# Decoder block on one core: quarter sums on VectorE, and another order of the first stage

## The chip, the core and the metric

The kernel runs on one core of a Trainium2 chip. A core has five engines with an instruction stream each: TensorE (PE, the matrix engine), VectorE (DVE), ScalarE (ACT), GpSimd (POOL) and SyncE (SP), which here only issues DMAs. Each stream runs in order, and the engines wait for each other through semaphores. Time is device time of one execution in microseconds (us); the figure given for a kernel is the median of its runs.

## The reference

One decoder block over 512 tokens and 1024 features, in float32:

```python
cs = silu(c)
mod = cs @ ada_w + ada_b                      # 6 x 1024: shift, scale, gate; twice
h = rmsnorm(x, norm_mix_g) * (1 + sc_m) + sh_m
q, k, v, g_ret, b, c_cv, u, g_a, g_b = split(h @ w_in)        # each 512 x 1024
q = rope(q, cos, sin); k = rope(k, cos, sin) * 128 ** -0.5    # 8 heads of 128
y_ret = head_layernorm(retention(q, k, v))
y_a = (silu(g_ret) * y_ret) @ ret_w_out
y_b = (b * conv3(c_cv * u)) @ conv_w_out
x = x + gt_m * ((sigmoid(g_a) * y_a + sigmoid(g_b) * y_b) @ mix_w_out)
h = rmsnorm(x, norm_ffn_g) * (1 + sc_f) + sh_f
x = x + gt_f * ((silu(h @ ffn_w_gate) * (h @ ffn_w_up)) @ ffn_w_down)     # 2816 wide
out = rmsnorm(x, final_norm_g)
```

`cos` and `sin` are those of position times inverse frequency; `rope` makes `t1 cos - t2 sin` and `t1 sin + t2 cos` of the two halves of a head.

## The kernel before

**Products.** Every float32 operand is split into a high part (a cast on ACT, names ending in `_h`) and the low rest (a subtraction on DVE, `_l`), and a product is three matmuls into one accumulator, low by high, high by low, high by high (`mm3`). A 128-feature column block of a projection, over 8 blocks of depth, is 24 matmuls of 512 columns. Its first matmul reads the low part of the weight, so it needs DVE's subtraction.

**Stages.** First stage: `x_load` brings four tiles of 128 tokens, `x_squares` sums their squares on ACT (Square, then Sqrt), `x_scaled` divides by the root on DVE and transposes on PE; `mod_row` multiplies pieces of `ada_w` by `cs` on PE, `ada_sum` does the same on DVE into `acc_m`, and `mod_sums` adds DVE's share on PE. From that come scale and shift for the first blocks of h, `Hh` and `Hl` (high and low). Then the products of c, u, b and the first k block run together, one depth block after another as the modulation becomes ready. Up to line 577 every engine's order is as written (`strict` in the class `InTurn`: each instruction is emitted after the one before on its engine).

After that come the projections of v, k, q and the ret gate with rotation and retention, one pair of heads (`p`) after another, then conv, output projections (`p_ya`, `p_yb`) with their gates (`p_ga`, `p_gb`), the mix, the FFN and the last norm. There a scheduler sets the order: it lists instructions by its own estimate of when their inputs will be there. `tc.issue_after` orders emission and with it the scheduler's estimate; it does not by itself put a wait between two engines.

**The rotation.** `rotary_steps` reduces position times frequency to a fraction of a turn in a chain of small DVE instructions (`fr`, `fy`); `rope_tables` makes `ropeC` and `ropeS` of it with eight Sin activations; `rope` takes each finished accumulator (`p_k`, `p_q`) and computes `a = p * C`, `b` in two halves of 64 rows, `a + b`, then the split in `_h` and `_l`. The positions are loaded on POOL's queue (lines 154 to 157).

**Sums over partitions.** In several places a sum over 128 partitions is left as four sums over 32 (`quarter_sums`, DVE's transposing reduction). `quart_sum` is a constant 0/1 matrix with which a small matmul adds the four quarters and spreads the result: `mod_quarters` (first stage), `mod_whole` (scale and shift of the FFN norm, between the output projections), and `gate_vec.spread` (the two gate vectors). Constants `quart_sum`, `quart_own` are made by `quarters`.

In the trace nearly all instructions go through `InTurn` and so bear its lines L62 (strict) and L64 (not strict).

Of the kernel before, what the change touches and what calls it, by code (L numbers as in the profile page):

```python
# [11 lines left out]
F32 = mybir.dt.float32  # L12
# [3 lines left out]
AF = mybir.ActivationFunctionType  # L16
ALU = mybir.AluOpType
AX = mybir.AxisListType

P = 128  # L20
S = 512
D = 1024
# [48 lines left out]
def block_kernel(ctx, tc, x, c, positions, ada_w, ada_b, norm_mix_g, w_in, conv_w, ret_w_out,  # L71
# [3 lines left out]
    pe, vec, act, pool, sync = (InTurn(tc, e) for e in (nc.tensor, nc.vector, nc.scalar, nc.gpsimd,  # L75
                                                        nc.sync))
# [13 lines left out]
    def scr(name, dt=F32, shape=None):  # L90
        return tp.tile(shape or [P, S], dt, tag="scr", bufs=12, name=name)
# [7 lines left out]
    def aux(name, shape=None):  # L99
        return ps.tile(shape or [P, S], F32, tag="aux", bufs=2, name=name)  # L100
# [30 lines left out]

    HS = S // 2
    c_sb = cp.tile([P, KT], F32, name="c_sb")
    sync.dma_start(c_sb, c.rearrange("o (p k) -> (o p) k", p=P))
    rows = cp.tile([P, P], F32, name="rows")
    vec.memset(rows, 0.0)
    R_ADA, R_GM, R_GF, R_CW = 0, 48, 56, 64
# [11 lines left out]
    with tc.issue_after(pool.last.ins):  # L149
        small.dma_start(rows[0:48], ada_b.rearrange("o (r p) -> (o r) p", p=P))  # L150
        small.dma_start(rows[48:56], norm_mix_g.rearrange("o (r p) -> (o r) p", p=P))
        small.dma_start(rows[56:64], norm_ffn_g.rearrange("o (r p) -> (o r) p", p=P))
        small.dma_start(rows[64:88], conv_w.rearrange("o t (r p) -> (o t r) p", p=P))
        for i in range(2):
            small.dma_start(posi[64 * i:64 * i + 64],
                            positions[0, HS * i:HS * (i + 1)].partition_broadcast(64))
        small.dma_start(ivf, inv_freq.rearrange("(f o) -> f o", o=1))
# [1 line left out]
    x2 = x[0].rearrange("(t p) (h n) -> t h p n", p=P, n=S)  # L159

    cs = cp.tile([P, KT], F32, name="cs")
    act.activation(cs, c_sb, AF.Silu)
    warm = cp.tile([P, 1], F32, name="warm")
    with tc.issue_after(act.last.ins):
        act.activation(warm, eps_t, AF.Sqrt)

    onesr = cp.tile([P, P], F32R, name="onesr")

# [2 lines left out]
    def rows_by_feature(tr):  # L171
        vecs.append(cp.tile([P, P], F32, name="vecs"))
        act.copy(vecs[0], tr[:, 0:P])
# [62 lines left out]
    QP = P // 4  # L236
    quart, own, mod_q = {}, {}, {}

    def quarters():
        quart["sum"] = cp.tile([P, 4, QP], F32, name="quart_sum")  # L240
        cols = sp.tile([P, QP], F32, tag="quart", bufs=1, name="quart_cols")
        vec.tensor_reduce(cols, ident.rearrange("p (q c) -> p c q", q=4), axis=AX.X, op=ALU.add)
        vec.tensor_copy(quart["sum"], cols.unsqueeze(1).to_broadcast([P, 4, QP]))
        quart["own"] = cp.tile([P, 4], F32, name="quart_own")
        vec.tensor_reduce(quart["own"], ident.rearrange("p (q c) -> p q c", q=4), axis=AX.X,
                          op=ALU.add)
        quart["f"] = cp.tile([P, 2 * D // QP], F32, name="quart_f")
# [10 lines left out]
        quarter_sums(quart["f"][:, j // 2 * n:(j // 2 + 1) * n], a)  # L258

    def mod_whole():  # L260
        pt = aux("mod_f")[:, 0:2 * D // QP]
        mm(pt, lhsT=quart["sum"].rearrange("p q c -> p (q c)"), rhs=quart["f"], start=True,
           stop=True)
        each = scr("mod_each")[:, 0:2 * D // QP].rearrange("p (n q) -> p n q", q=4)
        vec.tensor_tensor(each, pt.rearrange("p (n q) -> p n q", q=4),
                          quart["own"].unsqueeze(1).to_broadcast([P, 2 * KT, 4]), ALU.mult)
        cols = sp.tile([P, KT // 2, 2, 2], F32, tag="quart", bufs=1, name="mod_cols")
        vec.tensor_reduce(cols.rearrange("p a s b -> p (a s b)"), each, axis=AX.X, op=ALU.add)
        a, b, s = (mod[f"{v}_f"].rearrange("p (a b) -> p a b", b=2) for v in "abs")
        g, r = (vecs[0][:, c:c + KT].rearrange("p (a b) -> p a b", b=2)  # L270
                for c in (R_GF, R_ADA + ADA["sh_f"] // P))
        vec.tensor_tensor(a, cols[:, :, 1], g, ALU.mult)
        vec.tensor_tensor(a, a, b, ALU.add)
        vec.tensor_tensor(s, cols[:, :, 0], r, ALU.add)
# [58 lines left out]
    def x_load():  # L333
        for t in range(NT):
            xt = wp.tile([P, 2, S], F32, tag="hi", name=f"x_{t}")
            xs[t] = [xt[:, h] for h in range(2)] + [xt.rearrange("p h n -> p (h n)")]
            load_raw.last = sync.dma_start(xs[t][2], x[0, t * P:(t + 1) * P, :])

    def w_load(k):
        for n in "cubk":  # L340
            cols = P if n == "k" else 2 * P
            w_raw[n, k] = scr(f"w_{n}0_{k}", F32, [P, 2, cols])
            load_raw.last = sync.dma_start(
                w_raw[n, k], wi[k * P:(k + 2) * P, COL[n]:COL[n] + cols].rearrange(
                    "(k p) n -> p k n", p=P))
# [17 lines left out]
    def x_squares(t):  # L363
        junk = scr(f"n1_{t}", BF16, [P, D])
        act.activation(junk, xs[t][2], AF.Square, accum_out=ssq[:, t:t + 1])
        act.activation(r4[:, t:t + 1], ssq[:, t:t + 1], AF.Sqrt, scale=1.0 / D, bias=eps_t)

    def x_scaled(t):
        r = r4[:, t:t + 1]
        vec.reciprocal(r, r)  # L370
        vec.tensor_scalar_mul(xs[t][2], xs[t][2], r)
        for h in range(2):
            txs[t, h] = acc(f"tx_{t}{h}").rearrange("p (k n) -> p k n", n=P)
            for k in range(4):
                transpose(txs[t, h][:, k], xs[t][h][:, k * P:(k + 1) * P], ident)
# [25 lines left out]
    busy(18)  # L401
    for t in range(2):
        x_squares(t)
    x_scaled(0)
    busy(3)
    x_squares(2)
# [3 lines left out]
    tr = pv("tr_rows")  # L410
    transpose(tr[:, 0:P], rows, ident)
    x_squares(3)
    rows_by_feature(tr)
    x_scaled(2)
    busy(1)
# [5 lines left out]
    x_by_feature(2, 0, act.copy)  # L421
    x_by_feature(2, 1, act.copy)
    mod_gains("m")
    quarters()
    mod_row(0, 1, apart, False)
    a = ada_sum(ada_raw["m", 0][2:6], 4 * P, "m0", None, 2)
    x_by_feature(3, 0, act.copy)
# [117 lines left out]
    for j in range(2, KT, 2):  # L545
        if j + 2 < KT:
            ada_load("m", j + 2)
            w_load(j + 2)
        steps = products(j - 1)
        run(steps, 14)  # L550
        if j == 2:
            mod_row(j, 7, both, True)
        else:
            some_sums(j, 4, KT)
        for n in "cubk":
            w_hi(n, j)
        if j < KT - 2:
            mod_sums(sums[j], both, j > 2)
            w_lo("c", j)
            mod_cols("m", j, mods.rearrange("p (i n) -> p i n", n=P)[:, :, 0])  # L560
        else:
            mod_quarters(j)
            w_lo("c", j)
            mod_own(j)
        for k in (j, j + 1):
            h_hi(k)
            h_full(k)
        for n in "ubk":
            w_lo(n, j)
        run(steps)  # L570
        some_sums(j + 2, 0, 2)
        h_lo(j)
        run(products(j))
        some_sums(j + 2, 2, 4)
        h_lo(j + 1)
# [316 lines left out]
    def gate_vec(name):  # L892
        gate[name] = [misc(f"{name}_{h}") for h in range(2)]
        bias = sp.tile([QP, QP], F32, tag="gbias", bufs=1, name=f"bias_{name}")
        nc.gpsimd.dma_start(
            bias, ada_b[0, ADA[name]:ADA[name] + D].rearrange("(j c) -> j c", c=QP))
        part = sp.tile([P, QP], F32, tag="gpart", bufs=1, name=f"part_{name}")

        def summed(j):
            raw = wp.tile([P, KT, 2 * P], F32, tag="raw", bufs=3, name=f"ada_{name}{j}")  # L900
            col = ADA[name] + 2 * j * P
            load_raw.last = nc.sync.dma_start(raw, aw[:, :, col:col + 2 * P])
            a = ada_sum([raw[:, k] for k in range(KT)], 2 * P, f"{name}{j}")
            n = 2 * P // QP
            quarter_sums(part[:, j * n:(j + 1) * n], a)

        def spread():

            pt = aux(f"gp_{name}")[0:QP, 0:QP]
            mm(pt, lhsT=quart["sum"][:, 0], rhs=part, start=True, stop=True)  # L910
            row = sp.tile([QP, QP], F32, tag="grow", bufs=1, name=f"row_{name}")
            vec.transpose(row, pt)
            vec.tensor_tensor(row, row, bias, ALU.add)
            line = dp.tile([QP, QP], F32, tag="gline", bufs=2, name=f"line_{name}")
            nc.gpsimd.dma_start(line, row)
            for h in range(2):
                nc.gpsimd.dma_start(
                    gate[name][h], line[h * QP // 2:(h + 1) * QP // 2].rearrange(
                        "j c -> (j c)").partition_broadcast(P))

        for j, n in enumerate((1, 3, 5, 6)):
            after(n, lambda j=j: summed(j))
        after(7, spread)
# [415 lines left out]
```

## Time and profile before

| | |
|---|---|
| median of 3 runs | 936.87 us (936.76 to 937.35) |
| profiled execution | 937.46 us, span of its trace 935.7 us |
| TensorE busy | 927.3 us, 4299 matmuls |
| VectorE busy | 623.9 us, 1001 instructions |
| ScalarE busy | 358.9 us, 531 instructions |
| GpSimd busy | 37.6 us, 72 instructions |
| HBM traffic | 139.91 MB read, 17.85 MB written |

How to read the lines that follow: a line of the timeline gives start, duration, engine, source line, operation, output and inputs with their shapes, and in brackets the idle time ahead of it and what ended it. A row of the windows gives the window, its length, then busy time (and instruction count) of PE, PE's weight loads, DVE, ACT and POOL, then the clock granted to PE (1.00 is full), the share of the DMA engines and GB/s. A row of the chain gives start, duration, engine and output. Consecutive matmuls overlap, so the distance of their starts (0.227 us for 512 columns, from 10.88 us for 48) is the price of one, not the 0.39 us of its row.

### The profile page before, as it was taken

How to read it: one execution, taken by the hardware profiler on the slowest of the kernel's cores; microseconds unless marked ns; L12 is line 12 of the kernel's file. 1: busy time of each engine (PE TensorE's matmuls, PEld its weight loads, DVE VectorE, ACT ScalarE, POOL GpSimd, SP SyncE). 2: the span in 40 equal slices, each digit the busy share in tenths (PEclk: the TensorE clock that was granted, in tenths of full speed). 3: DMA queues.
4: the chain of work that ended last, by engine and by line, in shares of the span. 5: the costliest groups of instructions: out<-in, count | busy, mean ns of one | idle time of the engine just before them, and what ended most of it. 6: DMA issues, size and time to landing. Idle time of an engine off the chain costs nothing.

```text
span 935.7 us, 11163 instructions
## 1 busy us (share of the span) xinstructions
PE 927.3 (99%) x4299; PEld 774.9 (83%) x4299; DVE 623.9 (67%) x1001; ACT 358.9 (38%) x531; POOL 37.6 (4%) x72
## 2 busy tenths in 40 slices
PE   8999999999999999999999999999999999999997
PEld 8888888888888888888888888988888888888886
DVE  5999784797868566654674457667665545566575
ACT  7534432544444333222233235423433223443324
POOL 2000000000001000000000000000011000001000
PEclk9999999999999999999999999999999999999999
DMA  9943423322463537765553552445578672368912
GB/s 324 338 156 107 136 73 102 102 72 98 153 218 102 180 103 244 215 203 191 170 190 113 180 181 89 136 152 190 198 248 269 225 255 72 102 168 233 334 63 90
DMA packets 119909, 158.49 MB, mean 169 GB/s; under 512 B 5476, under 2 KB 94864, under 8 KB 118704
## 3 DMA queue, kind: packets, MB, share of 16 engines
q1 hardware_dynamic: 114672, 139.61, 45.3%
q0 software_dynamic: 5040, 18.04, 6.0%
q8 instruction: 33, 0.54, 0.2%
q14 instruction: 20, 0.16, 0.1%
q10 hardware_dynamic: 144, 0.13, 0.0%
HBM read 139.91 MB, written 17.85 MB: 169 GB/s over the span
## 4 chain that ended last, share of the span: by engine, by line
PE 96%; DVE 1%; ACT 1%; DMA 1%; SPq 0%; issue 0%; DVEq 0%
PE p_fu L64 13%; PE p_fg L64 12%; PE dn_t L64 5%; PE p_g L64 5%; PE p_yb L64 5%; PE p_gb L64 5%; PE p_q L64 5%; PE p_v L64 5%; PE p_ya L64 5%; PE p_ga L64 5%; PE p_k L64 4%; PE dn_b L64 4%; PE p_b L64 4%; PE p_u L64 4%; PE p_c L64 3%; PE mix L64 3%
## 5 line engine op out<-in xcount | busy, mean ns | idle before, releaser
L64 PE MATMUL p_fu<-Gh,w_fu_l 128*128 128x512 f32 x160 | 62.4, 390 | 0.0
L64 PE MATMUL p_fu<-Gh,w_fu_h 128*128 128x512 f32 x160 | 62.3, 389 | 0.0
L64 PE MATMUL p_fu<-Gl,w_fu_h 128*128 128x512 f32 x160 | 62.2, 389 | 0.0
L64 PE MATMUL p_fg<-Gh,w_fg_l 128*128 128x512 f32 x160 | 62.2, 389 | 0.0
L64 PE MATMUL p_fg<-Gl,w_fg_h 128*128 128x512 f32 x160 | 62.2, 389 | 0.0
L64 PE MATMUL p_fg<-Gh,w_fg_h 128*128 128x512 f32 x160 | 62.2, 389 | 0.0
L64 DVE TENSOR_TENSOR w_bl<-w_bl 128x512 f32<-128x512 f32 x36 | 24.8, 688 | 26.7 <-DMA w_bl<-in_ffn_w_down_dram 26.4
L64 ACT CAST w_fu_h<-w_fu 128x1024 fp32r<-128x1024 f32 x20 | 21.0, 1054 | 56.2 <-PE p_fu L64 33.3
L64 DVE TENSOR_TENSOR w_fg_l<-w_fg,w_fg_h 128x1024 fp32r<-128x1024 f32 x20 | 24.3, 1219 | 25.3 <-ACT w_fg_h L64 25.2
L64 DVE TENSOR_TENSOR w_b_l<-w_b,w_b_h 128x1024 fp32r<-128x1024 f32 (+1 forms) x21 | 24.0, 1146 | 22.2 <-ACT w_b_h L64 22.1
L64 ACT ACTIVATE fg<-p_fg 128x512 f32<-128x512 f32 x22 | 13.1, 598 | 62.5 <-PE p_fg L64 62.5
L64 PEld LDWEIGHTS p_fu<-Gh,w_fu_h 128*128 128x128 f32 x160 | 30.0, 188 | 6.3
L64 PEld LDWEIGHTS p_fg<-Gh,w_fg_h 128*128 128x128 f32 x160 | 30.0, 188 | 6.3
L64 PEld LDWEIGHTS p_fu<-Gh,w_fu_l 128*128 128x128 f32 x160 | 30.0, 188 | 6.2
L64 PEld LDWEIGHTS p_fg<-Gh,w_fg_l 128*128 128x128 f32 x160 | 30.0, 188 | 6.2
L64 PEld LDWEIGHTS p_fg<-Gl,w_fg_h 128*128 128x128 f32 x160 | 30.0, 188 | 6.2
L64 PEld LDWEIGHTS p_fu<-Gl,w_fu_h 128*128 128x128 f32 x160 | 30.0, 188 | 6.2
L64 DVE TENSOR_TENSOR fg<-p_fu,fg 128x512 f32<-128x512 f32 x22 | 15.2, 690 | 27.8 <-PE p_fu L64 27.8
L64 DVE TENSOR_TENSOR w_t_l<-w_t,w_t_h 128x1024 fp32r<-128x1024 f32 (+1 forms) x20 | 22.2, 1115 | 13.9 <-ACT w_t_h L64 13.8
L64 ACT CAST w_t_h<-w_t 128x1024 fp32r<-128x1024 f32 (+1 forms) x20 | 19.4, 968 | 25.5 <-PE dn_t L64 12.7
L64 ACT CAST w_b_h<-w_b 128x1024 fp32r<-128x1024 f32 (+1 forms) x21 | 20.8, 989 | 20.4 <-issue 7.9
L64 ACT CAST sh<-sm 128x512 fp32r<-128x512 f32 (+3 forms) x32 | 14.7, 460 | 35.3 <-DVE sm L64 35.2
(438 smaller groups left out, 2713.3 us busy)
## 6 DMA issues: line engine op xcount, KB each, us to landing
w_fg<-in_ffn_w_gate_dram SPq DMA_DIRECT2D x11, 1024.0 KB, 5.5
w_fu<-in_ffn_w_up_dram SPq DMA_DIRECT2D x11, 1024.0 KB, 5.8
w_bl<-in_ffn_w_down_dram SPq DMA_DIRECT2D x18, 512.0 KB, 4.7
blocks<-w_bl POOLq DMA_DIRECT2D x9, 1024.0 KB, 5.2
ada_m<-in_ada_w_dram SPq DMA_DIRECT2D x32, 256.0 KB, 5.4
ada_f<-in_ada_w_dram SPq DMA_DIRECT2D x32, 256.0 KB, 4.2
w_t<-blocks SPq DMA_DIRECT2D x8, 1024.0 KB, 5.6
w_b<-in_ffn_w_down_dram SPq DMA_DIRECT2D x6, 1024.0 KB, 5.0
```

What stands on the lines that cost most here:

```text
L64: self.last = op(*args, **kw)
```

## The change

It does these things:

- The load of `c` goes from the head of SP's queue to behind the four loads of x.
- The Silu of `c` (`cs`) goes from ahead of the Sqrt warm-up on ACT to behind the fourth `x_squares`.
- The loads of positions and inverse frequencies go into a function that is called in the last turn of the first-stage loop, after the last `Hh` in emission.
- `quarters()`, which makes the constants, goes from behind `mod_gains("m")` to ahead of the first `x_scaled`.
- In `mod_whole` the small matmul is replaced by copies between partition quarters and two additions on DVE (a butterfly: neighbouring quarters, then halves).
- In `gate_vec.spread` it is replaced by four copies and a reduction on DVE. `mod_quarters` keeps its matmul.

```diff
--- before.py
+++ after.py
@@ -131,7 +131,6 @@
 
     HS = S // 2
     c_sb = cp.tile([P, KT], F32, name="c_sb")
-    sync.dma_start(c_sb, c.rearrange("o (p k) -> (o p) k", p=P))
     rows = cp.tile([P, P], F32, name="rows")
     vec.memset(rows, 0.0)
     R_ADA, R_GM, R_GF, R_CW = 0, 48, 56, 64
@@ -151,6 +150,8 @@
         small.dma_start(rows[48:56], norm_mix_g.rearrange("o (r p) -> (o r) p", p=P))
         small.dma_start(rows[56:64], norm_ffn_g.rearrange("o (r p) -> (o r) p", p=P))
         small.dma_start(rows[64:88], conv_w.rearrange("o t (r p) -> (o t r) p", p=P))
+
+    def rotary_loads():
         for i in range(2):
             small.dma_start(posi[64 * i:64 * i + 64],
                             positions[0, HS * i:HS * (i + 1)].partition_broadcast(64))
@@ -159,10 +160,8 @@
     x2 = x[0].rearrange("(t p) (h n) -> t h p n", p=P, n=S)
 
     cs = cp.tile([P, KT], F32, name="cs")
-    act.activation(cs, c_sb, AF.Silu)
     warm = cp.tile([P, 1], F32, name="warm")
-    with tc.issue_after(act.last.ins):
-        act.activation(warm, eps_t, AF.Sqrt)
+    act.activation(warm, eps_t, AF.Sqrt)
 
     onesr = cp.tile([P, P], F32R, name="onesr")
 
@@ -258,9 +257,12 @@
         quarter_sums(quart["f"][:, j // 2 * n:(j // 2 + 1) * n], a)
 
     def mod_whole():
-        pt = aux("mod_f")[:, 0:2 * D // QP]
-        mm(pt, lhsT=quart["sum"].rearrange("p q c -> p (q c)"), rhs=quart["f"], start=True,
-           stop=True)
+        pt, moved = quart["f"], scr("mod_moved")[:, 0:2 * D // QP]
+        for n in (QP, 2 * QP):
+            for p0 in range(0, P, n):
+                p1 = p0 ^ n
+                vec.tensor_copy(moved[p0:p0 + n], pt[p1:p1 + n])
+            vec.tensor_tensor(pt, pt, moved, ALU.add)
         each = scr("mod_each")[:, 0:2 * D // QP].rearrange("p (n q) -> p n q", q=4)
         vec.tensor_tensor(each, pt.rearrange("p (n q) -> p n q", q=4),
                           quart["own"].unsqueeze(1).to_broadcast([P, 2 * KT, 4]), ALU.mult)
@@ -335,6 +337,7 @@
             xt = wp.tile([P, 2, S], F32, tag="hi", name=f"x_{t}")
             xs[t] = [xt[:, h] for h in range(2)] + [xt.rearrange("p h n -> p (h n)")]
             load_raw.last = sync.dma_start(xs[t][2], x[0, t * P:(t + 1) * P, :])
+        sync.dma_start(c_sb, c.rearrange("o (p k) -> (o p) k", p=P))
 
     def w_load(k):
         for n in "cubk":
@@ -401,6 +404,7 @@
     busy(18)
     for t in range(2):
         x_squares(t)
+    quarters()
     x_scaled(0)
     busy(3)
     x_squares(2)
@@ -410,6 +414,7 @@
     tr = pv("tr_rows")
     transpose(tr[:, 0:P], rows, ident)
     x_squares(3)
+    act.activation(cs, c_sb, AF.Silu)
     rows_by_feature(tr)
     x_scaled(2)
     busy(1)
@@ -421,7 +426,6 @@
     x_by_feature(2, 0, act.copy)
     x_by_feature(2, 1, act.copy)
     mod_gains("m")
-    quarters()
     mod_row(0, 1, apart, False)
     a = ada_sum(ada_raw["m", 0][2:6], 4 * P, "m0", None, 2)
     x_by_feature(3, 0, act.copy)
@@ -546,6 +550,9 @@
         if j + 2 < KT:
             ada_load("m", j + 2)
             w_load(j + 2)
+        else:
+            with tc.issue_after(hist[-1].ins):
+                rotary_loads()
         steps = products(j - 1)
         run(steps, 14)
         if j == 2:
@@ -906,8 +913,11 @@
 
         def spread():
 
-            pt = aux(f"gp_{name}")[0:QP, 0:QP]
-            mm(pt, lhsT=quart["sum"][:, 0], rhs=part, start=True, stop=True)
+            four = scr(f"four_{name}", F32, [QP, 4, QP])
+            for q in range(4):
+                vec.tensor_copy(four[:, q], part[q * QP:(q + 1) * QP])
+            pt = sp.tile([QP, QP], F32, tag="gsum", bufs=1, name=f"sum_{name}")
+            vec.tensor_reduce(pt, four.rearrange("p q j -> p j q"), axis=AX.X, op=ALU.add)
             row = sp.tile([QP, QP], F32, tag="grow", bufs=1, name=f"row_{name}")
             vec.transpose(row, pt)
             vec.tensor_tensor(row, row, bias, ALU.add)
```

What this moves on the engines. On DVE, around the rotation tables of the first pair of heads, where `v03` is the fourth v tile, `w_q00_l` and `w_q01_l` are the low parts of the first two q weights, `w_g00_l` that of the first gate weight, `k00`/`k01`/`q00`/`q01` the rotated blocks; the order before is

```order
L64 TENSOR_TENSOR w_q00_l_939<-w_q0_935,w_q00_h_937 128x1024
L64 TENSOR_TENSOR v03_c_870<-p_v03_842,v03_m_867 128x512
L64 TENSOR_TENSOR w_q01_l_978<-w_q0_935,w_q01_h_976 128x1024
L64 TENSOR_TENSOR v03_l_873<-v03_c_870,v03_h_872 128x512
L64 TENSOR_TENSOR w_g00_l_1023<-w_g0_1019,w_g00_h_1021 128x1024
L64 TENSOR_TENSOR k00_a_884<-p_k00_123,ropeC_738 128x512
L64 TENSOR_TENSOR k00_b_885<-p_k00_123,ropeS_739 64x512 x2
L64 TENSOR_TENSOR k01_a_925<-p_k01_900,ropeC_738 128x512
L64 TENSOR_TENSOR k00_a_884<-k00_a_884,k00_b_885 128x512
L64 TENSOR_TENSOR k01_b_926<-p_k01_900,ropeS_739 64x512 x2
```

and of the change

```order
L64 TENSOR_TENSOR w_q00_l_939<-w_q0_935,w_q00_h_937 128x1024
L64 TENSOR_TENSOR v03_c_870<-p_v03_842,v03_m_867 128x512
L64 TENSOR_TENSOR k00_a_884<-p_k00_118,ropeC_738 128x512
L64 TENSOR_TENSOR k00_b_885<-p_k00_118,ropeS_739 64x512
L64 TENSOR_TENSOR v03_l_873<-v03_c_870,v03_h_872 128x512
L64 TENSOR_TENSOR k00_b_885<-p_k00_118,ropeS_739 64x512
L64 TENSOR_TENSOR k01_a_925<-p_k01_900,ropeC_738 128x512
L64 TENSOR_TENSOR k00_a_884<-k00_a_884,k00_b_885 128x512
L64 TENSOR_TENSOR k01_b_926<-p_k01_900,ropeS_739 64x512 x2
L64 TENSOR_TENSOR k00_l_891<-k00_a_884,k00_h_890 128x512
L64 TENSOR_TENSOR k01_a_925<-k01_a_925,k01_b_926 128x512
L64 TENSOR_TENSOR q00_a_966<-p_q00_941,ropeC_738 128x512
```

followed by

```order
L64 TENSOR_TENSOR q00_b_967<-p_q00_941,ropeS_739 64x512 x2
L64 TENSOR_TENSOR k01_l_932<-k01_a_925,k01_h_931 128x512
L64 TENSOR_TENSOR q00_a_966<-q00_a_966,q00_b_967 128x512
L64 TENSOR_TENSOR w_q01_l_978<-w_q0_935,w_q01_h_976 128x1024
L64 TENSOR_TENSOR q00_l_973<-q00_a_966,q00_h_972 128x512
L64 TENSOR_TENSOR w_g00_l_1023<-w_g0_1019,w_g00_h_1021 128x1024
```

`w_q01_l`, the second of the two, stood ahead of all rotations and now stands behind those of both k blocks and of the first q block. Of these rows the ones on `v03` and `w_q00_l` lead in both, and so do the rows ahead of them.

On PE, at the end of the first q block (`p_q00`) and the start of the second (`p_q01`), before:

```order
L64 MATMUL p_q00_941<-Hl_116,w_q00_h_937 128x512
L64 MATMUL p_q00_941<-Hh_115,w_q00_h_937 128x512
L64 MATMUL p_q01_980<-Hh_115,w_q01_l_978 128x512
L64 MATMUL p_q01_980<-Hl_116,w_q01_h_976 128x512
L64 MATMUL p_q01_980<-Hh_115,w_q01_h_976 128x512
```

and of the change:

```order
L64 MATMUL p_q00_941<-Hl_111,w_q00_h_937 128x512
L64 MATMUL p_q00_941<-Hh_110,w_q00_h_937 128x512
L64 MATMUL st0_0_1085<-q00_h_972,k00_l_891 128x512
L64 MATMUL p_q01_980<-Hh_110,w_q01_l_978 128x512
L64 MATMUL p_q01_980<-Hl_111,w_q01_h_976 128x512
L64 MATMUL p_q01_980<-Hh_110,w_q01_h_976 128x512
```

The first product of the first scores (`st0_0`, of the rotated q and k) has moved ahead of the second q block.

On ACT at the start, before:

```order
L64 ACT_TABLE_LOAD
L64 ACTIVATE cs_97<-c_sb_75 128x8
L64 ACT_TABLE_LOAD
L64 ACTIVATE warm_99<-eps_t_79 128x1
L62 ACTIVATE n1_0_169,ssq_121<-x_0_125 128x1024
...
L62 ACTIVATE n1_3_211,ssq_121<-x_3_131 128x1024
L62 ACTIVATE r4_122<-ssq_121,eps_t_79 128x1
L62 COPY vecs_214<-tr_rows_209 128x128
L62 COPY xT_0_117<-tx_10_195 128x2x128
```

and of the change:

```order
L64 ACT_TABLE_LOAD
L64 ACTIVATE warm_94<-eps_t_78 128x1
L62 ACTIVATE n1_0_165,ssq_116<-x_0_120 128x1024
...
L62 ACTIVATE n1_3_214,ssq_116<-x_3_126 128x1024
L62 ACTIVATE r4_117<-ssq_116,eps_t_78 128x1
L62 ACT_TABLE_LOAD
L62 ACTIVATE cs_93<-c_sb_75 128x8
L62 COPY vecs_218<-tr_rows_212 128x128
L62 COPY xT_0_112<-tx_10_198 128x2x128
```

There is one table load less at the start, and one now stands between the fourth square and `vecs`, with `cs` behind it. Two later ones, ahead of the first `ropeC` and ahead of the first gate activation, are gone: the set that `cs` leaves loaded is used there. On POOL the loads of the positions stand at the same place as before, behind those of `rows`, and have no wait.

## The prediction

> **What bounds the kernel now.** I read the page's first part, then the chain of waits, then the timeline at the places that the change touches.
>
> ```profile
> span 935.7 us, 11163 instructions
> PE 927.3 (99%) x4299; PEld 774.9 (83%) x4299; DVE 623.9 (67%) x1001; ACT 358.9 (38%) x531; POOL 37.6 (4%) x72
> ```
>
> TensorE (PE) is the bound: 935.7 − 927.3 leaves 8.4 us without a matmul, most of it before the first product of the first stage (19.64 us) and after the last matmul (930.03 us). Between the two PE has no slack, so whatever makes it wait there, or gives it more to do, lengthens the run one for one. VectorE (DVE) at 67% looks harmless, but that is a mean. The windows around the rotary steps:
>
> ```profile
> 60.00:70.00 10.00, 10.00 (x46) 8.29 (x45) 9.69 (x24) 0.00 (x0) 0.00 (x0) 1.00 0.55 194
> ...
> 80.00:88.70 8.70, 8.70 (x40) 7.19 (x39) 8.70 (x18) 8.10 (x13) 0.00 (x0) 1.00 0.37 121
> 88.70:94.30 5.60, 5.60 (x26) 4.66 (x25) 5.51 (x9) 2.33 (x5) 0.00 (x0) 1.00 0.71 237
> ```
>
> The third figure after the comma is DVE's busy time: 9.69 of 10.00 us, 8.70 of 8.70, 5.51 of 5.60. DVE has no hole there, so the order of its instructions decides when PE gets its operands.
>
> **The change, part by part.**
>
> *(1) DVE's order at the rotation, the main term.* The diff places the loads of the positions later in the program, and the listed order shows what the scheduler made of that: the position rows stand on POOL where they stood, with no wait, but on DVE the low half of the second q weight (`w_q01_l`, in the trace the second `w_q_l`; operand of the first matmul of `p_q01`) now stands behind the rotation of k and of the first q instead of ahead of it. On DVE and PE before:
>
> ```profile
> 84.93 0.44 DVE L62 TENSOR_SCALAR fr<-fr 128x512 f32<-128x512 f32 x1
> 85.93 1.24 DVE L64 TENSOR_TENSOR w_q_l<-w_q,w_q_h 128x1024 fp32r<-128x1024 f32 x1
> 87.06 0.71 DVE L64 TENSOR_TENSOR v_c<-p_v,v_m 128x512 f32<-128x512 f32 x1
> 87.66 1.24 DVE L64 TENSOR_TENSOR w_q_l<-w_q,w_q_h 128x1024 fp32r<-128x1024 f32 x1
> ...
> 90.53 0.71 DVE L64 TENSOR_TENSOR k_a<-p_k,ropeC 128x512 f32<-128x512 f32 x1
> 91.26 1.39 DVE L64 TENSOR_TENSOR k_b<-p_k,ropeS 64x512 f32<-64x512 f32 x2
> 92.68 0.69 DVE L64 TENSOR_TENSOR k_a<-p_k,ropeC 128x512 f32<-128x512 f32 x1
> 93.28 0.68 DVE L64 TENSOR_TENSOR k_a<-k_a,k_b 128x512 f32<-128x512 f32 x1
> ...
> 93.92 0.39 PE L64 MATMUL p_q<-Hh,w_q_h 128*128 128x512 f32 x1
> 94.14 0.39 PE L64 MATMUL p_q<-Hh,w_q_l 128*128 128x512 f32 x1
> ```
>
> The second `w_q_l` was done at 88.90 and first used at 94.14, the first matmul of `p_q01`: 5.2 us early. Behind the rotation it is late. First the rotary tables on ScalarE (ACT):
>
> ```profile
> 84.47 0.61 ACT L64 CAST v_h<-v_c 128x512 fp32r<-128x512 f32 x1
> 85.10 1.28 ACT L64 ACT_TABLE_LOAD   x1
> 86.39 0.42 ACT L64 ACTIVATE ropeC<-fr 64x256 f32<-64x256 f32 x1
> 86.71 0.40 ACT L64 ACTIVATE ropeS<-fr 64x256 f32<-64x256 f32 x1
> 87.13 0.42 ACT L64 ACTIVATE ropeC<-fr 64x256 f32<-64x256 f32 x1
> ```
>
> The change has no table load here and puts the eight activations in a row. They can start when `fr` is done (84.93 + 0.44, so about 85.40), a C/S pair takes 87.13 − 86.39 = 0.74, and the last `ropeC` ends at about 88.03. DVE's waiting `k_a` starts at 88.08. From start to start the rows give 0.60 for an instruction behind an unrelated one, about 0.72 where the second reads the first, 1.42 for a pair of 64-row products, 1.24 for `w_q_l` alone. Ahead of `w_q_l` now stand: k_a, k_b, v_l, k_b (0.72 + 0.71 + 0.72 + 0.71 = 2.86), then k_a, the k_a addition, k_b twice (0.60 + 0.72 + 1.42 = 2.74), then k_l, addition, q_a, q_b twice, k_l, addition (0.60 + 0.60 + 0.72 + 1.42 + 0.60 + 0.60 = 4.54). 88.08 + 10.14 = 98.22 for its start, 99.46 for its end. The q_a in between reads all of `p_q00`, complete at 93.92 + 0.39 = 94.31, and is due at 94.88: no further wait. PE resumes at about 99.50 instead of 94.14: 5.36. The first score product, which the order moves ahead of `p_q01`, waits for ACT's q_h (near 98.98) and fills 0.23 of that: it is no longer to be done later. About 0.1 for restarting gives **+5.2**. Bounds: the fastest intervals everywhere (0.60, pairs at 1.39) give 4.4; half a microsecond of extra waiting between ACT and DVE gives 5.8. What is queued behind the late `w_q_l` on DVE (q_l, w_g_l, w_k_l) is needed only after `p_q01`'s 24 matmuls (24 × 0.22 = 5.3 us), so no second stall follows.
>
> *(2) The first stage.*
>
> ```profile
> 0.74 0.39 SPq L64 DMA_DIRECT2D c_sb<-in_c_dram  x1
> 1.19 1.84 SPq L62 DMA_DIRECT2D x<-in_x_dram  x4
> ...
> 2.59 1.28 ACT L64 ACT_TABLE_LOAD   x1
> 3.88 0.20 ACT L64 ACTIVATE warm<-eps_t 128x1 f32<-128x1 f32 x1
> ...
> 7.19 1.06 ACT L62 ACTIVATE n<-x 128x1024 bf16<-128x1024 f32 x1 [0.75 <-DMA x<-in_x_dram]
> ...
> 12.04 0.29 ACT L62 ACTIVATE r<-ssq,eps_t 128x1 f32<-128x1 f32 x1
> 12.24 0.24 ACT L62 COPY vecs<-tr_rows 128x128 f32<-128x128 f32 x1
> ...
> 16.74 0.62 ACT L62 CAST w_c_h<-w_c 128x512 fp32r<-128x512 f32 x1 [1.41 <-DMA w_c<-in_w_in_dram]
> ...
> 12.44 0.39 PE L62 MATMUL mods<-cs,ada_m 128*128 128x128 f32 x2
> ...
> 17.47 0.89 PE L62 MATMUL mods<-ones,acc_m 128*128 128x128 f32 x4 [0.26 <-DVE acc_m L62]
> ...
> 19.64 0.73 PE L62 MATMUL p_c<-Hh,w_c_h 128*128 128x512 f32 x2
> ```
>
> The loads of x are issued 1.19 − 0.74 = 0.45 earlier, and since ACT waits for x, its squares move by about 0.45. But the table load and the Silu of c now stand behind the fourth square: 12.33 + 1.28 + 0.2 is 13.85, less 0.45 is 13.40, where PE, in its own order, could begin the `mods` products at 12.4. Their chain ran without holes to about 17.1; 1.5 − 0.45 later it ends at 18.2, against the 17.47 at which the sums of `acc_m` begin. DVE's `acc_m` waits for the same Silu but has lost 0.8 us of constants ahead of it, so PE's order is the later. Queued on ACT behind the Silu are `vecs` and ten copies of `xT`; they have the 1.41 us of hole before `w_c_h`. The load of c passes four loads of x on SP and still has some ten microseconds until the Silu; the loads behind it keep their place, fifth and later. 18.2 − 17.47 = **+0.7**, and everything from the first product (19.64) on moves along. Bounds: no gain of x, +1.2; x gaining twice 0.45, +0.3.
>
> In the Trainium skill, "ScalarE: Activation LUTs", section "What ACT_TABLE_LOAD costs", a switch of sets is 1.28 us of load and 1.38 of drain. The load agrees with the rows (1.28), but the activation starts 0.01 after it (3.88), so no drain shows; with one, this term would by an estimate from that page be +2.1.
>
> *(3) The small products.*
>
> ```profile
> 506.62 0.18 PE gp_gt_m L64 x2
> 664.27 0.18 PE gp_gt_f L64 x2
> 446.51 0.17 PE mod_f L64 x2
> ```
>
> These rows of the chain leave PE: **−0.6** with the slower first matmul behind each (lower bound the plain 0.53, upper 0.7). In their place DVE does copies and additions on tiles of at most 64 columns, which by the first row below (0.19 for 32 by 32) I put at 0.25 each; six copies and two additions come to 2 us, and they stand in holes such as that of the second row:
>
> ```profile
> 507.27 0.19 DVE L64 STREAM_TRANSPOSE row_gt_m<-gp_gt_m 32x32 f32<-32x32 f32 x1
> ...
> 437.23 1.23 DVE L64 TENSOR_TENSOR w_gb_l<-w_gb,w_gb_h 128x1024 fp32r<-128x1024 f32 x1 [4.21 <-ACT w_gb_h L64]
> ```
>
> Were the cover gone, they would cost PE their 2 us once, and about 1.2 (four copies and a reduction) at each of the two gate vectors.
>
> Sum: 5.2 + 0.7 − 0.6 = +5.3. The profiled execution took 937.46 (its span and 1.8 around it), 0.6 over the median 936.87; on it the sum gives 942.8, on the median **942.2**.
>
> **The rivals.**
>
> *The clock drops in the gap (33%).* The new hole of PE is 4.5 us without a matmul (94.6 to 99.0). What the clock does without matmuls shows at the end:
>
> ```profile
> 928.00:930.00 2.00, 2.00 (x17) 1.82 (x16) 1.87 (x7) 1.88 (x6) 0.00 (x0) 1.00 0.73 280
> 930.00:932.00 2.00, 0.03 (x1) 0.00 (x0) 1.49 (x6) 1.38 (x5) 0.00 (x0) 1.00 0.67 258
> 932.00:934.00 2.00, 0.00 (x0) 0.00 (x0) 0.43 (x2) 0.19 (x1) 0.00 (x0) 0.93 0.60 217
> 934.00:935.70 1.70, 0.00 (x0) 0.00 (x0) 0.00 (x0) 0.00 (x0) 0.00 (x0) 0.50 0.15 58
> ```
>
> Granted clock (third from the end) 0.93 in 932–934 and 0.50 after: half speed from about 933.7 (0.07 of the window's 2 us lost at half clock is 0.28 us), some 3.7 us after the last matmul. A hole of 4.5 us is long enough for that, but not always. If PE then runs at half speed for 2 to 3.5 us after the hole, it loses half of that: +1 to +1.7, giving 943.2 to 943.9; twice as long, 945.5. By the Trainium skill, "TensorE: Matmul & The Clock Gate", Part 1, the activity window is free-running and 3.41 us long, so by an estimate a hole of 4.5 holds a whole window in (4.5 − 3.41)/3.41, about a third of the cases; the fall at 3.7 us agrees.
>
> *Not slower (7%).* The stall exists only if DVE runs the listed rows in that order and `w_q_l` ends after 94.1. If the rotation were 5.4 us earlier or `w_q_l` ahead of it, terms 2 and 3 alone remain: 936.9 + 0.7 − 0.6 = 937.0, and with x gaining more than thought 936.5. Against it: before, DVE's trace followed its list row by row, and the ten microseconds of work ahead of `w_q_l` are measured durations; the rotary chain before them is full.
>
> *The positions are late in truth (2%).* If their loads waited for the last Hh, the rotary chain on a full DVE would move back by the wait, and the stall with it: 1 us late is 943.2. Against it is that no wait stands before the rows on POOL.
>
> *The stall is smaller than worked out (4%):* if the ACT-to-DVE handovers overlap better or the tables start earlier, 4 us, 940.9.
>
> **How the numbers follow.** My own case, the stall with the clock kept, has 54%, and 941.3 to 943.1 is its range. A third goes to the clock, so the range reaches up to 944.4 and leaves out its doubled form; downward it ends at 940.9 (the 4.4 us of the bound with the first stage at +0.3), leaving the 7% of no stall outside. A measurement of this kernel tells 0.2%, 1.9 us, from no change. Slower: 54 + 33 + 2 + 4 = 93%, same 5% (no stall), faster 2% (no stall, and a first stage that gains well over a microsecond).
>
> **What would show it.** Right: on PE one hole of about 4.5 us behind the first q projection, released by ACT's q_h and then DVE's `w_q_l`; the first product of the first stage near 20.3; no table load at the ropes; total PE idle near 14. Wrong: `p_q01` following `p_q00` without a hole, or a hole released by a DMA; the first product at or before 19.6 (term 2); PE's clock under 1.00 in the window from 97 to 104 (then the rival); a wait on PE at 446, 506 or 664 for DVE (term 3's cover).

## The result, and the profile after

The changed kernel takes 943.75 us (942.77 to 944.16, six executions) against 937.12 us (936.76 to 937.69, six) of the kernel before: ratio 1.0070, 95% interval 1.0060 to 1.0081. It is slower by 6.6 us, where 942.2 was forecast in a range of 940.9 to 944.4. The profiled execution took 944.00 us, its span is 942.2 us. From the page:

```profile
span 942.2 us, 11167 instructions
PE 929.1 (99%) x4293; PEld 776.6 (82%) x4293; DVE 628.6 (67%) x1019; ACT 356.3 (38%) x529; POOL 37.6 (4%) x72
```

TensorE's idle time has gone from 8.4 to 13.1 us, and its busy time has grown by 1.8 us with six matmuls fewer. The second cannot come from the work; it is a slower clock. The place is where the first q block ends. PE's timeline:

```profile
93.68 0.39 PE L64 MATMUL p_q<-Hh,w_q_h 128*128 128x512 f32 x1
98.71 0.80 PE L64 MATMUL st<-q_h,k_l 128*128 128x512 f32 x1 [4.64 <-ACT q_h L64]
99.31 0.75 PE L64 MATMUL p_q<-Hh,w_q_l 128*128 128x512 f32 x1
99.85 0.63 PE L64 MATMUL p_q<-Hl,w_q_h 128*128 128x512 f32 x1
...
104.97 0.41 PE L64 MATMUL p_q<-Hl,w_q_h 128*128 128x512 f32 x1
105.22 0.40 PE L64 MATMUL p_q<-Hh,w_q_h 128*128 128x512 f32 x1
...
107.50 0.39 PE L64 MATMUL p_g<-Hh,w_g_l 128*128 128x512 f32 x1
```

The brackets name the hole, 4.64 us, and what ended it. Behind it the starts of matmuls lie 0.43 us apart until 105, not 0.227. The windows of one microsecond show why (PE's granted clock is the third figure from the end):

```profile
97.00:98.00 1.00, 0.00 (x0) 0.00 (x0) 1.00 (x3) 0.00 (x0) 0.00 (x0) 1.00 0.00 0
98.00:99.00 1.00, 0.29 (x1) 0.29 (x1) 1.00 (x2) 0.62 (x1) 0.00 (x0) 0.59 0.00 0
99.00:100.00 1.00, 1.00 (x3) 0.65 (x3) 1.00 (x3) 0.00 (x0) 0.00 (x0) 0.50 0.00 0
...
104.00:105.00 1.00, 1.00 (x4) 0.71 (x4) 0.00 (x0) 0.00 (x0) 0.00 (x0) 0.50 1.07 377
105.00:106.00 1.00, 1.00 (x6) 0.83 (x5) 0.00 (x0) 0.00 (x0) 0.00 (x0) 1.00 1.08 376
```

Half clock from about 98.2 (0.59 is 0.18 us of full and 0.82 of half) to 105.0. DVE's timeline shows the late operand:

```profile
85.71 1.21 DVE L64 TENSOR_TENSOR w_q_l<-w_q,w_q_h 128x1024 fp32r<-128x1024 f32 x1
86.84 0.68 DVE L64 TENSOR_TENSOR v_c<-p_v,v_m 128x512 f32<-128x512 f32 x1
87.80 0.69 DVE L64 TENSOR_TENSOR k_a<-p_k,ropeC 128x512 f32<-128x512 f32 x1 [0.28 <-ACT ropeC L64]
...
97.32 0.69 DVE L64 TENSOR_TENSOR q_a<-q_a,q_b 128x512 f32<-128x512 f32 x1
97.92 1.22 DVE L64 TENSOR_TENSOR w_q_l<-w_q,w_q_h 128x1024 fp32r<-128x1024 f32 x1
```

The second `w_q_l` ends at 99.14, not at 88.90. The first stage, on ACT and PE:

```profile
11.07 0.29 ACT L62 ACTIVATE r<-ssq,eps_t 128x1 f32<-128x1 f32 x1
11.38 1.28 ACT L62 ACT_TABLE_LOAD   x1
12.68 0.21 ACT L62 ACTIVATE cs<-c_sb 128x8 f32<-128x8 f32 x1
...
12.94 0.49 PE L62 MATMUL mods<-cs,ada_m 128*128 128x128 f32 x2 [1.06 <-ACT cs L62]
...
17.49 0.61 PE L62 MATMUL mods<-ones,acc_m 128*128 128x128 f32 x4
...
19.39 0.73 PE L62 MATMUL p_c<-Hh,w_c_h 128*128 128x512 f32 x2
```

A ledger from the starts of the same products in both profiled executions:

| start of | before | after | difference | what came since the row above |
|---|---|---|---|---|
| first product of c | 19.64 | 19.39 | −0.25 | first stage |
| first q block | 88.70 | 88.47 | −0.23 | nothing |
| first gate block | 99.58 | 107.50 | +7.92 | hole and half clock, +8.15 |
| second pair's k block (chain) | 111.31 | 119.00 | +7.69 | a score product done earlier, −0.23 |
| first `p_yb` | 457.50 | 464.91 | +7.41 | `mod_f` gone, −0.28 |
| mix | 534.08 | 541.07 | +6.99 | `gp_gt_m` gone, −0.42 |
| first `dn_b` | 669.96 | 676.50 | +6.54 | `gp_gt_f` gone, −0.45 |
| span | 935.7 | 942.2 | +6.5 | nothing |

The 8.15 splits by the second q block: it took 107.50 − 99.31 = 8.19 us where 24 matmuls take 5.44, so 2.75 is the clock and 5.40 the wait. The 5.40 includes the score product, which took 0.60 us at half clock (98.71 to 99.31).

### The profile page after: what moved, and what is told of

It reads as the page before. It is cut to its first block, busy times and chain, and to the rows that moved or that the text cites. A ratio compares the mean times of both kernels' runs of the same rounds, so it can differ in the third digit from the quotient of the medians.

```text
span 942.2 us, 11167 instructions
## 1 busy us (share of the span) xinstructions
PE 929.1 (99%) x4293; PEld 776.6 (82%) x4293; DVE 628.6 (67%) x1019; ACT 356.3 (38%) x529; POOL 37.6 (4%) x72
## 4 chain that ended last, share of the span: by engine, by line
PE 90%; DVE 5%; ACT 2%; DMA 1%; issue 1%; SPq 0%; DVEq 0%
PE p_fu L64 13%; PE p_fg L64 12%; PE dn_t L64 5%; PE p_g L64 5%; PE p_yb L64 5%; PE p_gb L64 5%; PE p_ya L64 5%; PE p_ga L64 5%; PE p_q L64 4%; PE dn_b L64 4%; PE p_k L64 3%; PE p_b L64 3%; PE p_u L64 3%; PE p_c L64 3%; PE mix L64 3%; PE p_v L64 2%
## 5 line engine op out<-in xcount | busy, mean ns | idle before, releaser
L64 DVE TENSOR_TENSOR w_t_l<-w_t,w_t_h 128x1024 fp32r<-128x1024 f32 (+1 forms) x20 | 22.2, 1114 | 13.1 <-ACT w_t_h L64 12.9
```

Source lines behind the costliest of these rows:

```text
L64: self.last = op(*args, **kw)
```

## The experiments

All times are medians, and each is set beside the kernel before on the same chip (937.0 to 937.2).

### Only the order on DVE undone

```diff
+        ks = proj(wi, COL["k"] + 2 * p * P, Hh, Hl, f"k{p}") if p else first_k()
+        qs = proj(wi, COL["q"] + 2 * p * P, Hh, Hl, f"q{p}")
+        if p == 0:
+            ks, qs = list(ks), list(qs)
-        for i, pt in proj(wi, COL["k"] + 2 * p * P, Hh, Hl, f"k{p}") if p else first_k():
+        for i, pt in ks:
             kk[i] = rope(pt, f"k{p}{i}")
-        for i, pt in proj(wi, COL["q"] + 2 * p * P, Hh, Hl, f"q{p}"):
+        for i, pt in qs:
             qq[i] = rope(pt, f"q{p}{i}")
```

> The change with one thing undone: the second q weight's low half is split ahead of the rotations again (k and q blocks of the first pair are all emitted before their rotations); Silu, loads of c and of the positions, constants and sums stay as in the change. Theory (the place of that split on DVE makes PE's hole, and the hole makes the half clock): no hole behind the first q block, clock 0.999, time 943.75 - 5.2 (hole, net of the score product) - 2.75 (half clock) = 935.8. Rival (the hole comes from later rotary tables or positions, whatever the order): a hole of 4 us or more and 943 to 944.

Measured: 936.50 us (935.81 to 936.75), ratio 0.9992 (0.9982 to 1.0001). On DVE and PE:

```profile
87.12 1.21 DVE L64 TENSOR_TENSOR w_q_l<-w_q,w_q_h 128x1024 fp32r<-128x1024 f32 x1
...
97.94 1.23 DVE L64 TENSOR_TENSOR w_g_l<-w_g,w_g_h 128x1024 fp32r<-128x1024 f32 x1
...
98.83 0.39 PE L64 MATMUL p_q<-Hh,w_q_h 128*128 128x512 f32 x1
99.32 0.47 PE L64 MATMUL p_g<-Hh,w_g_l 128*128 128x512 f32 x1
```

No hole behind the first q block, and 7.2 us less than the change: its loss hung on this order. Of the 0.7 us above my 935.8, a quarter of a microsecond is explained: this order puts the first gate weight's split late in its turn, it ends at 99.17, and PE starts the gate block 0.49 after the start of its last matmul, not 0.23. The other 0.45 stays open. The first stage is the same in both kernels, but its first product comes anywhere from 18.86 to 19.75 in the eight traces that have it, so executions scatter by more than this.

### Positions at their old place

```diff
+    with tc.issue_after(pool.last.ins):
+        rotary_loads()
...
-        else:
-            with tc.issue_after(hist[-1].ins):
-                rotary_loads()
```

> The change with the loads of positions and inverse frequencies back at their old place, all else as in the change. The reading on record (the late place of these loads is what the scheduler answered with the new DVE order): the order of before comes back, no hole, 935.8. Rival (the scheduler answers to the table load that is gone ahead of the rotary activations, because the late Silu leaves its set loaded): the DVE order of the change stays, hole of 4.6 us, half clock in most executions, 943.0 to 944.2.

Measured: 942.88 us (942.53 to 943.96), ratio 1.0063 (1.0048 to 1.0078). PE, and the windows around the fall of the clock:

```profile
98.15 0.79 PE L64 MATMUL st<-q_h,k_l 128*128 128x512 f32 x1 [4.62 <-ACT q_h L64]
```

```profile
93.00:94.00 1.00, 0.53 (x3) 0.11 (x1) 1.00 (x2) 0.39 (x1) 0.00 (x0) 1.00 0.00 0
...
95.00:96.00 1.00, 0.00 (x0) 0.00 (x0) 0.99 (x2) 0.18 (x1) 0.00 (x0) 0.83 0.00 0
...
102.00:103.00 1.00, 1.00 (x5) 0.83 (x4) 0.59 (x1) 0.00 (x0) 0.00 (x0) 0.76 1.09 388
```

The hole is still there. The late positions are not needed for it, and the reading in my prediction, that the scheduler answered to them, is refuted. The windows tell something else too. The clock falls at 95.66 (0.83), only 2.1 us after the last matmul (93.53), and returns at 102.5, some 6.8 us later. Since it fell early in the hole, less of the half-speed time met work. The 3.4 us that end at the fall (92.25 to 95.66) still hold 1.28 us of matmuls.

### Silu and c early again, positions late

```diff
+    sync.dma_start(c_sb, c.rearrange("o (p k) -> (o p) k", p=P))     # head of the queue
...
+    act.activation(cs, c_sb, AF.Silu)
+    with tc.issue_after(act.last.ins):
+        act.activation(warm, eps_t, AF.Sqrt)
-    act.activation(warm, eps_t, AF.Sqrt)
...
-        sync.dma_start(c_sb, c.rearrange("o (p k) -> (o p) k", p=P))     # behind x
...
-    act.activation(cs, c_sb, AF.Silu)                                 # behind x_squares(3)
```

> The change with c at the head of SP's queue and Silu ahead of the Sqrt warm-up again; positions late, constants first and sums on DVE as in the change. Theory (the late Silu, by the table load it spares ahead of the rotary activations, is what made the scheduler list the rotations first): the table load is back ahead of the ropes, the second q weight's low half is ahead of the rotations, no hole, 937.02 - 1.26 = 935.8 (935.4 to 936.1). Reading on record (the late positions cause the order): hole of 4.6 us or so, 942.5 to 944.

Measured: 935.75 us (935.49 to 935.88), ratio 0.9984 (0.9975 to 0.9994). ACT and DVE:

```profile
84.66 1.28 ACT L64 ACT_TABLE_LOAD   x1
85.96 0.42 ACT L64 ACTIVATE ropeC<-fr 64x256 f32<-64x256 f32 x1
```

```profile
87.22 1.20 DVE L64 TENSOR_TENSOR w_q_l<-w_q,w_q_h 128x1024 fp32r<-128x1024 f32 x1
...
88.95 1.21 DVE L64 TENSOR_TENSOR w_g_l<-w_g,w_g_h 128x1024 fp32r<-128x1024 f32 x1
90.09 0.67 DVE L64 TENSOR_TENSOR k_a<-p_k,ropeC 128x512 f32<-128x512 f32 x1
```

With Silu back, its table load is back ahead of the ropes, and the q weight is ahead of the rotations. So it is a move made 70 us earlier and on another engine that set the order on DVE. This edit takes back the place of Silu and that of the load of c together, and no run takes back one alone in the scheduler's own order. Silu is the likelier of the two: with Silu early and c loaded from ACT's queue (below) there is no hole either, and with c at the head and Silu late (below) no table load stands ahead of the ropes. That the link is the spared table load (the scheduler expects the rotations 1.3 us sooner and lists them first) fits every kernel here: those with a load ahead of the ropes have the old order, those without have the new one unless it is forced. It was not tried alone and is not shown.

### The hole filled

```diff
+            pt = acc(f"p_{name}{i}")
+            if (name, i) == ("q0", 1):
+                for _ in range(18):
+                    mm(pt, lhsT=wh[:, 0, :], rhs=Ah[:, 0, :], start=True, stop=True)
-            yield i, fm_gemm(acc(f"p_{name}{i}"), wh, wl, Ah, Al)
+            yield i, fm_gemm(pt, wh, wl, Ah, Al)
```

> The change, with 18 spare matmuls (128x512) put into the hole behind the first q block: they write the accumulator of the second q block, whose own first matmul starts it afresh, so nothing else changes. 18 x 0.227 = 4.1 of the 4.64 us are filled. Theory (the half clock comes from PE's idle hole): clock 0.999, 943.75 - 2.75 = 941.0, the wait for the low half being unchanged. Rival (the clock falls for another reason near there, or the spare matmuls run into the wait and push it): 943.5 to 944.5.

Measured: 941.18 us (940.89 to 941.35), ratio 1.0042 (1.0026 to 1.0059).

```profile
98.82 0.68 PE L64 MATMUL st<-q_h,k_l 128*128 128x512 f32 x2 [0.56 <-ACT q_h L64]
```

```profile
98.00:99.00 1.00, 0.43 (x3) 0.18 (x2) 1.00 (x2) 0.62 (x1) 0.00 (x0) 1.00 0.00 0
99.00:100.00 1.00, 1.00 (x5) 0.72 (x6) 1.00 (x3) 0.00 (x0) 0.00 (x0) 1.00 0.00 0
```

The wait for `w_q_l` is as long as it was, but PE is never idle for long, keeps its clock, and the run is 2.6 us shorter with 18 matmuls more. The price of the half clock is shown by itself, and the rest of the change is +4.0 us.

### How long a hole has to be to cost the clock

The same edit with 5, 9 and 13 spare matmuls.

> The change, with 5 spare matmuls in the hole: 5 x 0.227 = 1.13 us filled, some 3.5 us of hole left. If a whole window of 3.41 us without matmuls is needed and its phase is free, the clock falls in about (3.5 - 3.41)/3.41, 3% of the executions: nearly all near 941.0 at 0.999. If a window that is mostly idle is enough: half clock in nearly all, 943 to 944.

> The change with 9 spare matmuls in the hole, 2.04 us filled, some 2.6 us of hole left (the runs with 4.6 and 3.5 us of hole lost the clock in every execution). If the clock needs a free-running window of 3.41 us without any matmul: never, 941.2 at 0.999. If a window about 60% idle is enough (the trace of the kernel with the positions back shows a fall after a window with 1.26 us of matmuls in it): half clock in about half of the executions, times split between 941 and 943, clocks between 0.995 and 0.999.

> The change with 13 spare matmuls in the hole, 2.95 us filled, some 1.7 us left, which is half of a 3.41 us window at most. If a window must be 60% idle or more: clock kept in all, 941.2. If less than that is enough: some executions at 942 to 943.5 with a lower clock.

| spare matmuls | hole, us | executions | clock below 0.998 in | median, us (range) |
|---|---|---|---|---|
| 0 | 4.64 | 6 | 6 | 943.75 (942.77 to 944.16) |
| 5 | 3.50 | 4 | 4 | 942.54 (942.20 to 943.86) |
| 9 | 2.58 | 4 | 3 | 942.98 (941.56 to 944.56) |
| 13 | 1.67 | 4 | 1 | 941.14 (940.89 to 942.83) |
| 18 | 0.56 | 4 | 0 | 941.18 (940.89 to 941.35) |

The clock in the fourth column is the mean over an execution; the kernel before and the filled one show 0.998 to 1.000 in every one. The holes from PE's timelines (5, 9 and 13), each with windows of its run:

```profile
98.75 1.11 PE L64 MATMUL st<-q_h,k_l 128*128 128x512 f32 x2 [3.50 <-ACT q_h L64]
...
98.00:99.00 1.00, 0.25 (x1) 0.26 (x2) 1.00 (x2) 0.62 (x1) 0.00 (x0) 0.50 0.00 0
104.00:105.00 1.00, 1.00 (x4) 0.80 (x3) 0.00 (x0) 0.00 (x0) 0.00 (x0) 0.59 1.08 386
```

```profile
99.02 0.83 PE L64 MATMUL st<-q_h,k_l 128*128 128x512 f32 x2 [2.58 <-ACT q_h L64]
...
99.00:100.00 1.00, 0.98 (x3) 0.79 (x4) 1.00 (x3) 0.00 (x0) 0.00 (x0) 0.68 0.00 0
102.00:103.00 1.00, 1.00 (x5) 0.77 (x4) 1.00 (x2) 0.00 (x0) 0.00 (x0) 0.61 1.09 387
```

```profile
99.02 0.67 PE L64 MATMUL st<-q_h,k_l 128*128 128x512 f32 x2 [1.67 <-ACT q_h L64]
...
99.00:100.00 1.00, 0.98 (x4) 0.75 (x5) 1.00 (x3) 0.00 (x0) 0.00 (x0) 1.00 0.00 0
```

A window of 3.41 us without a matmul (the length in the Trainium skill, "TensorE: Matmul & The Clock Gate", Part 1) does not fit into 2.58 us, and by the mean clocks the clock fell in three of four executions, of which one has a trace. With a hole of 2.58 the half clock lasted from 99.36 to 102.78, 3.4 us. With 3.50 it lasted from 98.0 to 104.82 (0.59), 6.8 us, as with 4.6. Either is a multiple of 3.4. A second stretch of 3.4 us came in the three traces in which it still held some of the hole (0.53 us of it in the change, 98.18 to 98.71). The one execution of four with 1.67 us of hole that took 942.83 has no trace; its mean clock is 0.997, but whether its hole was as short stays open.

### The sums alone

```diff
@@ mod_whole and gate_vec.spread as in the change, all else as in the kernel before
```

> The kernel before with the DVE sums alone (mod_whole and spread as in the change, all else as before). Theory (each small product cost its own matmuls and a slower start of the product behind it; 0.2 to 0.3 for mod_f, 0.4 for each gate vector by the starts of the products around them in the two traces; DVE's additions lie in holes): 937.17 - 1.07 = 936.1. The prediction's own term was 0.6: 936.55. Rival (DVE's additions come on the path): 937 or more.

Measured: 935.76 us (935.37 to 936.51), ratio 0.9988 (0.9979 to 0.9997): −1.26 us, twice the 0.6 of the prediction. The chain shows where it lies, first before, then the change:

```profile
501.18 5.44 PE p_yb L64 x24
506.62 0.18 PE gp_gt_m L64 x2
506.80 5.68 PE p_yb L64 x24
```

```profile
508.60 10.88 PE p_yb L64 x48
```

The small product's own row is 0.18, but the 24 matmuls behind it took 5.68, not 5.44: 0.42 in all, as in the ledger. Why those behind it take longer is not shown.

### The first stage alone

```diff
@@ the order-kept kernel with both small products back on TensorE
-        pt, moved = quart["f"], scr("mod_moved")[:, 0:2 * D // QP]
...
+        pt = aux("mod_f")[:, 0:2 * D // QP]
+        mm(pt, lhsT=quart["sum"].rearrange("p q c -> p (q c)"), rhs=quart["f"], ...)
```

> The first stage alone: the order-kept kernel with the small products back on TensorE, so x first, c and Silu later, constants first, and no hole at the second q block. It carries 0.24 us of wait for the gate weight's low half that its forced order brought. Theory (x first gains about what the late Silu costs): first product of the first stage at 19.1 to 19.6, time 937.17 + 0.24 + (-0.25 to +0.2) = 937.2 to 937.6. The prediction's term (+0.7): 938.1.

Measured: 937.36 us (937.02 to 937.93), ratio 1.0004 (0.9995 to 1.0013). Less the quarter of a microsecond of the forced order, the first stage is worth +0.1. From the order-kept kernel (−0.67 to its kernel before, of which −1.26 are the sums and +0.24 the order) it is +0.35. By the traces it is nothing: the first product of c comes at 19.41 in the mean of eight traces with the change's first stage (18.86 to 19.75), and at 19.39 in that of three with c at the head of SP's queue and Silu early (19.22, 19.31 and 19.64). So it is small and not told from nothing, but not +0.7.

### c at the head again, Silu late

```diff
+    sync.dma_start(c_sb, c.rearrange("o (p k) -> (o p) k", p=P))     # head of the queue
...
-        sync.dma_start(c_sb, c.rearrange("o (p k) -> (o p) k", p=P))     # behind x
@@ rest as in the order-kept kernel
```

> The order-kept kernel (936.5) with the load of c back at the head of SP's queue, Silu still late. If c ahead of x costs x its issue alone: squares and cs 0.45 later, first product 0.45 later, 936.95. If its 128 small packets also slow the start of x: about 0.96 later, 937.4. If x's arrival does not bound the late cs: 936.5.

Measured: 936.81 us (936.22 to 937.35), ratio 0.9998 (0.9989 to 1.0007). Against its kernel before it is −0.21, the order-kept one −0.67: 0.46 for c ahead of x. That is what its issue takes on SP (1.19 − 0.74). The intervals overlap, and the traces say more. The first product, in the order-kept kernel and then here:

```profile
19.12 0.73 PE L62 MATMUL p_c<-Hh,w_c_h 128*128 128x512 f32 x2
```

```profile
20.03 0.73 PE L62 MATMUL p_c<-Hh,w_c_h 128*128 128x512 f32 x2
```

That is 0.91. Over all traces the root of the fourth square (`r`) starts at 10.54 to 11.43 with c behind x (eight traces) and at 11.66 to 12.04 with c ahead of it on SP (four): 0.70 between the means. So c ahead of x costs x something, more than its issue by the traces, and the size is open between 0.46 and 0.91.

### c from ACT's queue, Silu early

```diff
+    act.dma_start(c_sb, c.rearrange("o (p k) -> (o p) k", p=P))
...
+    with tc.issue_after(act.last.ins):
+        act.activation(cs, c_sb, AF.Silu)
...
-    act.activation(cs, c_sb, AF.Silu)                                 # behind x_squares(3)
@@ positions at their old place; sums and constants as in the change
```

> Another first stage: x first on SP, c loaded by ACT's own queue, Silu of c early again (ahead of the Sqrt warm-up), constants first, sums on DVE, positions at their old place. The Sin and gate table loads come back and with them, by the theory, the DVE order of before: no hole at the second q block. Expected: x gains up to 0.96 and nothing waits for a late cs, so the first product comes 0.5 to 1.2 earlier than before; with 1.07 of the sums 937.17 - 1.07 - 0.9 = 935.2 (934.9 to 935.6). Rival (c's packets slow x from any queue): 936.1, as the sums alone.

Measured: 935.68 us (935.60 to 935.73), ratio 0.9986 (0.9977 to 0.9995). The half microsecond hoped for beyond the sums did not come. ACT here, then `cs` in the kernel before:

```profile
4.48 0.21 ACT L64 ACTIVATE cs<-c_sb 128x8 f32<-128x8 f32 x1 [2.02 <-DMA c_sb<-in_c_dram]
4.70 1.28 ACT L64 ACT_TABLE_LOAD   x1
...
6.11 1.04 ACT L62 ACTIVATE n<-x 128x1024 bf16<-128x1024 f32 x1
```

```profile
2.36 0.21 ACT L64 ACTIVATE cs<-c_sb 128x8 f32<-128x8 f32 x1 [0.34 <-DMA c_sb<-in_c_dram]
```

Issued at 0.74 beside x, c was there only at 4.48; from the head of SP's queue Silu had it at 2.36. Silu and the table load behind it then held up the first square to 6.11. What x gained, c lost. This kernel and the two others that beat the kernel before clear of the noise (the sums alone, and Silu early with the sums) lie within 0.1 us of each other: no run here won more than the sums.

## Why the prediction was right, and where not

**Direction, place and the mechanism of the wait were right.** `w_q_l` was to end at 99.46 and PE to resume at 99.50; with everything 0.25 earlier by the first stage, it ended at 99.14 and PE resumed at 99.31, a little later than at full clock, since the score product ahead of it ran at half speed. The hole was put at 4.5 and was 4.64; the wait, less the score product, was put at 5.2 and was 5.40 − 0.23 = 5.17. Summing the starts of DVE's rows from its old trace in their new order was enough, since that stretch of DVE has almost no slack. Undoing the order alone took it all back.

**The cause of the order was wrong.** The prediction ascribed the new DVE order to the late loads of the positions. With these back at their old place the hole stays (942.88); with Silu and c back it goes (935.75). The number did not hang on it, because the order itself was read, but advice drawn from it would have undone the wrong line.

**The likeliest case was not the one that came.** I gave the half clock 33% and kept it out of the 942.2. It came in all six executions. Two of the prediction's own signs of being wrong were there: a clock under 1.00 between 97 and 104, and a first product at or before 19.6 (it came at 19.39). The step that failed is "a hole of 4.5 us is long enough for that, but not always", with the third that followed from asking for a whole window without matmuls. The runs show the clock falling in three of four with a hole of 2.58, so a window with a good part of matmuls in it counts as idle. With the positions back it fell after 3.4 us of which 1.28 were matmuls and 2.13 were not. A hole of 4.64 leaves at least half of itself, 2.32, in one of two neighbouring stretches of that length, so by an estimate from this trace it cannot miss. By the rule of the Trainium skill ("TensorE: Matmul & The Clock Gate", Part 1) that I used, at least one idle window is needed; the length and the free phase agree with the traces (a half-speed stretch of 3.4 us, or of twice that), but idle does not mean empty here. The price was mis-sized too: +1.0 to +1.7 for a single window, where 2.75 was measured, since the half clock lasted 6.8 us: the second 3.4 us of it still held 0.53 of the hole. That was the "twice as long" form, priced at 945.5 and left out of the range.

**Two terms were off in the same direction.** With the clock kept, my 942.2 stands against 941.18. The small products were put at −0.6 and are −1.26 by the time, −1.15 by the ledger: I counted their own rows and almost nothing for the products behind them. The first stage was put at +0.7 and is +0.1 to +0.35. Its mechanism was there (the table load and Silu behind the fourth square, PE waiting 1.06 for `cs`), but PE began at 12.94 and not at 13.40: the squares ended 0.97 earlier than in the trace of before, not 0.45. Part of that trace was late by chance: the kernel with the sums alone, whose first stage is that of before, had its first product at 19.31, not 19.64. The prediction also took the wait for `acc_m` at 17.47 as the only one. The four products of that row took 0.89 before and 0.61 after, so about 0.27 more of waiting went away. These two errors of about 1 us together and the missing 2.75 of clock went against each other. That the total still fell inside the range is luck: 942.2 + 2.75 would be 944.95, above the 944.4 at which the range ends.

**The covers held.** DVE's additions in the place of the small products cost nothing that can be seen, as the sums alone show, and no later stall appeared behind the late `w_q_l`.

## What to carry to other kernels

Where a scheduler sets the order, a moved line can change it on an engine and at a time that have no part in the move: read the new order wherever that engine has no slack, price it with durations of the old trace, and let single edits undone say which line caused it. A hole of 2.6 us or more between matmuls cost half of the clock for 3.4 or 6.8 us in most executions here, beside its own length, and spare matmuls in it win that part back (2.6 us here). A tiny product between large ones can cost more than its row (0.42 for 0.18 here), so take its price from the starts of the products around it.

## What the runs showed of the hardware that was not expected

By the mean clocks, the clock fell with holes of 2.58 us in three of four executions and once of four with 1.67, and in one trace it fell after only 2.1 us without a matmul. Half clock lasted 3.4 us in one trace and 6.8 us in three. The four executions with a hole of 2.58 spread over 3.0 us, where 33 of the kernel before spread over 1.3. The arrival of x scatters too: in eight traces with the same order of loads on SP the root of the fourth square starts at 10.54 to 11.43. The 4 KB load of c, issued at 0.74 from ACT's queue beside the 2 MB of x, was usable at 4.48 us; from the head of SP's queue, ahead of x, at 2.36.
